# The second bias tile of the attention requested beside the first, and the weight sums of the up pairs built in other halves and one split ahead of their casts

## The chip, the cores and the metric

The kernel runs on one core of one Trainium2 chip. The metric is device time in microseconds (us) of one launch on the slowest core, which here is the only core; several launches are timed and the median is taken. Beside the timed launches one execution is recorded by the hardware profiler, and every duration below that is not a median comes from that execution.

## What is computed

One inference step of a two-layer encoder trunk for 1024 prompt tokens and 32 sample tokens, all in fp32. Layer 0 mixes with an mLSTM, layer 1 with a windowed attention that has a distance bias and one learned sink for each head; after each stands a SwiGLU block, and after each block a layer norm. Cut to what the change touches:

```python
def swiglu(x, w_gu, w_down):
    g, u = jnp.split(x @ w_gu, 2, axis=-1)
    return (jax.nn.silu(g) * u) @ w_down

def sink_attention(q, k, v, sinks, bias):
    s = jnp.einsum('bcqhgd,bckhd->bchgqk', q, k).astype(F32) * (HEAD_DIM ** -0.5) + bias
    sk = sinks.astype(F32).reshape(N_KV_HEADS, GROUP)[:, :, None, None]
    mx = jnp.maximum(jnp.max(s, -1, keepdims=True), sk)
    p = jnp.exp(s - mx)
    p = p / (jnp.sum(p, -1, keepdims=True) + jnp.exp(sk - mx))
    return jnp.einsum('bchgqk,bckhd->bcqhgd', p.astype(v.dtype), v)

def trunk(...):
    ...
        x = layer_norm(DEEPNORM_ALPHA * x + mix, ln_g[layer, 0], ln_b[layer, 0])
        x = layer_norm(DEEPNORM_ALPHA * x + swiglu(x, w_gu[layer], w_down[layer]), ln_g[layer, 1], ln_b[layer, 1])
```

The model width is 1024, the hidden width of SwiGLU 2816 (22 tiles of 128), and there are 16 query heads of 64.

## The kernel before, in words

**Layout and products.** Activations lie transposed: 128 features on the partitions, the 1056 tokens as columns. An fp32 product is made of three TensorE (PE) matmuls: each operand is split into a rounded high part and a low part, and `gemm` (L360) adds high times high (L368), high times low (L369) and low times high (L370) in PSUM.

**Weights.** The class `Weights` (L129) turns weights into such high and low parts. It walks one fixed list of jobs. `load_to` (L156) asks for a raw unit of 128x1024 (tile `wr`, four buffers) by a DMA from SyncE's queue (SP, L162). A job splits one half of a unit: ScalarE (ACT) casts it to the high part (tile `wh`, L208), and GpSimd (POOL), or for some units VectorE (DVE), subtracts to get the low part (tile `wl`, L210). Five pairs of buffers hold the parts. When a product has been issued, `done` (L234) frees its parts and issues the next job, so that four halves stand split or in work ahead of PE.

**The up product.** Of each SwiGLU's 22 hidden tiles, two are done plainly and 20 (`up_tile`, L1342) by a scheme that saves one product in eight: two raw units `a` and `b` (gate and up weights, each with halves 1 and 2) go into seven factors, and each factor is multiplied with an operand of its own (`x11`, `x21`, `t1` to `t4`, `x22`). The factors are a1, a2, b2, s1 = b1 + b2, s2 = s1 - a1, s3 = a1 - b1 and s4 = a2 - s2. Their job order is a1, a2, b2, s2, s1, s3, s4; PE takes them as a1, a2, s2, b2, s1, s3, s4. Four sums of 128x512 on DVE make s1 to s4 in place in the two raw tiles (`_source`, L166): at the job of b2 one (L176), at s2 two (L179 and L180), at s1 one (L182). Each is issued with the job that casts it, and DVE takes its instructions in order. The products go to two PSUM banks A and two B in turn; ACT copies A out (L1362, L1372, L1379, L1390), DVE adds B (L1367, L1375, L1382 to L1384). A product that goes on adding to A waits for the copy before it. The down product's pairs use the same code.

**Staging.** After every second hidden tile a task `stage` (L1278) forms the operands of the down product: DVE sums (L1300, L1301, L1306, L1313), ACT casts (L1288), DVE or POOL subtracts (L1289), SP stores 528 KB to DRAM (L1290, `hs_x` and `hs_t`). There are two buffers for it, so the third cast of a stage waits for the first store.

**Attention.** Eight pairs of heads j visit nine blocks b of 128 tokens. `scores` (L1707) multiplies queries and keys into two PSUM banks `psS` (L1719, L1720), and DVE adds the bias (L1725), whose tile `bt` carries the sink in its last column. ACT takes the exponential (L1737), DVE the reciprocal (L1741), POOL scales (L1743), PE transposes (L1763), ACT and DVE split the result (L1766, L1767), PE multiplies with the values (L1778, L1779). `load_bias` (L1649) asks for the bias of a head pair (two DMAs from SP, L1653 and L1654: 256 KB and a small one) and copies the sinks into it (POOL, L1655 and L1656). The first tile is asked for when the keys begin; each further one when the visit before it begins, with two buffers in turn. The visits are 0, 1, 2, 3 and then 0 to 7.

**Order.** No scheduler reorders anything: each engine runs its instructions in the order in which the code records them, and waits there for what they need. Tasks (`Weave`, L70) are recorded between matmuls by estimated times that stand in the code. SP's queue holds the loads of weights, the stores of the stages, and the copies that spread keys and queries over partitions (L1589 to L1593, L1630, L1631), all in order. Each DMA also waits for the DMA eight before it to land, since eight semaphores are used in turn.

Of the kernel before, what the change touches and what calls it, by code (L numbers as in the profile page):

```python
# [30 lines left out]
FT = D_FF // P  # L31
# [3 lines left out]
FIRST, TAIL = 2, 4  # L35
# [34 lines left out]
class Weave:  # L70


    def __init__(self):
        self.tasks = []
        self.feed = None
# [53 lines left out]
class Weights:  # L129
# [7 lines left out]
    def __init__(self, nc, pool, units, pairs, on_vector):  # L137
        self.nc, self.pool, self.units, self.on_vector = nc, pool, units, on_vector
        self.nload = self.njob = 0
        self.raw, self.parts, self.home, self.live = {}, {}, {}, set()  # L140
        self.jobs, self.last = [], {}
        self.wait, self.ahead, self.pause = 0.0, False, FEED_W
        self.depth = RAW - 1
        self.spare, self.spared = None, set()
        u = 0
        while u < len(units):
            if u in pairs:
                self.jobs += [(u, f) for f in self.FACTORS]
                self.last[u] = self.last[u + 1] = len(self.jobs) - 1
                u += 2  # L150
            else:
                self.jobs += [(u, 0), (u, 1)]
                self.last[u] = len(self.jobs) - 1
                u += 1
# [11 lines left out]
    def _source(self, u, f):  # L166

        n = self.units[u].shape[-1] // 2
        if f in (0, 1):
            return self.raw[u][:, f * n : (f + 1) * n]  # L170
        sub, add = self.nc.vector.tensor_sub, self.nc.vector.tensor_add
        a, b = self.raw[u], self.raw[u + 1]
        a1, a2, b1, b2 = a[:, :n], a[:, n : 2 * n], b[:, :n], b[:, n : 2 * n]
        if f == "b2":

            sub(a1, a1, b1)  # L176
        elif f == "s2":

            add(b1, b1, b2)  # L179
            sub(b2, b2, a1)  # L180
        elif f == "s1":
            sub(a2, a2, b2)  # L182
        return {"a1": a1, "a2": a2, "b2": b2, "s1": b1, "s2": b2, "s3": a1, "s4": a2}[f]

    def _next(self):
        if self.njob == len(self.jobs):
            return False
        key = self.jobs[self.njob]
        u, f = key
        if key not in self.home and len(self.live) == SLOTS and (self.spared or not self.spare):  # L190
            return False
        if key in self.home and any(self.home.get(k) is self.home[key] for k in self.parts):
            return False
        self.load_to(u if f in (0, 1) else u + 1)
        r = self._source(u, f)
        w = r.shape[-1]
        if key in self.home:
            hi, lo = self.home[key]
        else:
            if self.spare and not self.spared:  # L200
                self.spared.add(key)
                at, tag, bufs = self.spare, "x", 1
            else:
                self.live.add(key)
                at, tag, bufs = self.pool, "", SLOTS
            hi = at.tile([P, WD // 2], F32R, name=f"wh{u}_{f}", tag="wh" + tag, bufs=bufs)[:, :w]
            lo = at.tile([P, WD // 2], F32R, name=f"wl{u}_{f}", tag="wl" + tag, bufs=bufs)[:, :w]
        self.nc.scalar.copy(hi, r)  # L208
        eng = self.nc.vector if key in self.on_vector else self.nc.gpsimd
        eng.tensor_sub(lo, r, hi.bitcast(F32))  # L210
        self.parts[key] = (hi, lo)
        self.njob += 1
        if f in (1, "s4"):
            del self.raw[u]
            if f == "s4":
                del self.raw[u + 1]
                u += 1
            self.load_to(u + self.depth)
        return True

    def split_to(self, i):
# [28 lines left out]
def kernel(ctx: ExitStack, tc: tile.TileContext, A, O):  # L250
# [14 lines left out]
    def new(p, tag, shape, dt=F32, bufs=1):  # L265
        uid[0] += 1
        return p.tile(list(shape), dt, name=f"{tag}_{uid[0]}", tag=tag, bufs=bufs)
# [27 lines left out]
    U_UP, U_DN = [], []  # L295
# [25 lines left out]
    on_vector.update((u, f) for u in U_O + U_OUT_A[0] + U_OUT_B[1] for f in range(2))  # L321
    on_vector.update((u, f) for u in U_Q[:1] for f in range(2))
    W = Weights(nc, base, units, pairs, on_vector)
    wv.feed = W.feed


# [52 lines left out]
    def tiles_of(half):  # L379

        hi, lo = half
        return [(hi[:, c : c + P], lo[:, c : c + P]) for c in range(0, hi.shape[-1], P)]

    def wcols(u):
        a, b = W.get(u)
        return tiles_of(a) + tiles_of(b)
# [245 lines left out]
    nc.scalar.preload_act_table_set("natural_log_exp_and_others")  # L632
    W.spare = pa
    eg = ExitStack()
# [943 lines left out]
    def k_part(src, c0, n):  # L1578

        dst = slice(c0, c0 + n)  # L1580
        nc.scalar.copy(KH[0][:, dst], src)
        nc.vector.tensor_sub(KL[0][:, dst], src, KH[0][:, dst].bitcast(F32))
# [63 lines left out]

    B = {}

    def load_bias(j):  # L1649
        at, bufs = (pb2, 1) if j == 5 else (pb, 2)  # L1650
        bt = new(at, "bt", [P, 2, 257], bufs=bufs)
        sb = new(at, "sb", [DEC, 2, 161], bufs=bufs)
        nc.sync.dma_start(bt[:, :, 0:256], A["bias"][:, 2 * j : 2 * j + 2, :])  # L1653
        nc.sync.dma_start(sb[:, :, 0:160], A["bias"][:DEC, 2 * j : 2 * j + 2, 0:160])  # L1654
        nc.gpsimd.tensor_copy(bt[:, :, 256], nsink[:, 2 * j : 2 * j + 2])  # L1655
        nc.gpsimd.tensor_copy(sb[:, :, 160], nsink[:DEC, 2 * j : 2 * j + 2])  # L1656
        B[j] = (bt, sb)

    load_bias(0)
    def keys_values(g):  # L1660
        if g == 2:
            k_part(ck[:], SEQ, P)
        for f, w in ((k_group, U_KV[g > 0][0]), (v_group, U_KV[g > 0][1])):
            f(g)
            if g != 1:
                W.done(w)
# [32 lines left out]
    ast = {"ready": 0, "scored": 0, "placed": 0, "v": 0, "visit": 0}  # L1699
    def attention(gap):  # L1700
        S = {}

        def window(b):

            return (P, 0) if b == 0 else (96, SEQ) if b == 8 else (0, (b - 1) * P)

        def scores(j, b):  # L1707
            _, t0, R, g, off = CH[b]
            if b == 0 or b == 3 and j < 4:
                ast["visit"] += 1  # L1710
                if ast["visit"] < len(visits):
                    load_bias(visits[ast["visit"]])
            s = S[j, b] = {}
            lo, k0 = window(b)
            q, g2, (bt, sb) = Q[j, g], j // 4, B[j]
            tk = slice(off, off + R)
            kc = slice(k0, k0 + 256 - lo)
            for h in range(2):
                nc.tensor.matmul(psS[h][:R, lo:256], q[:, h, tk], KH[g2][:, kc], start=True, stop=False)  # L1719
                nc.tensor.matmul(psS[h][:R, lo:256], q[:, h, tk], KL[g2][:, kc], start=False, stop=True)  # L1720
            p = s["p"] = new(pb2, "s", [P, 2, 257], bufs=4)
            st = s["st"] = new(pb2, "st", [P, 3, 2], bufs=6)
            bias = sb[:, :, :] if b == 8 else bt[:, :, lo:257]
            for h in range(2):
                nc.vector.tensor_tensor_reduce(  # L1725
                    p[:R, h, lo:257], psS[h][:R, lo:257], bias[:R, h], 1.0, 3e38,
                    op0=ALU.add, op1=ALU.min, accum_out=st[:R, 0, h : h + 1],
                )
            ast["scored"] += 1
# [53 lines left out]
        def place(j, b):  # L1783
# [4 lines left out]
            for h in range(2):  # L1788
# [22 lines left out]
    visits = [*range(4), *range(8)]  # L1811
# [6 lines left out]
    for g in range(1, 3):  # L1818
        keys_values(g)
        wv.launch(v_turn(g, 2.5))  # L1820
# [177 lines left out]
```

## Time and profile before

| | us |
|---|---|
| median of three timed launches | 2218.43 (2216.13 to 2218.95) |
| the profiled execution: its own time | 2219.82 |
| the profiled execution: span of its instructions | 2218.0 |
| TensorE busy in the span | 2178.0 |
| VectorE, ScalarE, GpSimd busy | 1468.7, 1002.6, 1020.5 |
| mean granted TensorE clock (1 is full) | 0.997 |
| up products of layer 0 and of layer 1, from and to | 521 to 931, 1554 to 1964 |
| attention, from and to | 1206 to 1427 |

Busy time is the time in which an engine executed an instruction; idle time is put down to what released the instruction that ended it. A row of a timeline gives start, duration, engine, line, operation, and output and inputs by the program's names with buffer numbers left out, then in brackets the engine's idle time before it and its releaser. A `q` behind an engine's name means its queue, where DMAs are issued. Matmuls follow each other in a pipeline, so the start of one to the start of the next counts, not the duration of one.

### The profile page before, as it was taken

Reading aid. Unit: us, or ns where it says so; the run is one execution under the profiler, and the core shown is the slowest. Engines: PE = TensorE matmul, PEld = TensorE weight load, DVE = VectorE, ACT = ScalarE, POOL = GpSimd, SP = SyncE. Lnnn points to the kernel's source line nnn. Section 1 sums busy time; section 2 is a strip of 40 time slices with the busy share of each in tenths; the row PEclk is TensorE's granted clock in tenths of the full one; section 3 lists DMA queues with packets and bytes.
Section 4 is the critical chain, followed back from the end, with each engine's and each line's share of the span. In section 5 each row is a group of like instructions: output and inputs, shape, how many; then the busy total and the mean of one; then the engine's idle time right before and its main releaser. Section 6 shows DMA issues by size and latency. Waiting matters only on the chain.

```text
span 2218.0 us, 44293 instructions
## 1 busy us (share of the span) xinstructions
PE 2178.0 (98%) x17086; PEld 2149.8 (97%) x17086; DVE 1468.7 (66%) x2848; ACT 1002.6 (45%) x2259; POOL 1020.5 (46%) x982
## 2 busy tenths in 40 slices
PE   9999999999999999999998999999999999999997
PEld 9999999999999999999998999899999999999997
DVE  4465677787666665566667678888576666466657
ACT  4443455464344444321245778756444444422125
POOL 2544210004666566544525776600576666554441
PEclk9999999999999999999999999999999999999999
DMA  5221212212443343797515333521244434397712
GB/s 169 78 62 57 57 39 86 89 39 80 153 155 136 137 155 136 248 333 230 175 57 173 108 100 97 155 63 39 103 162 163 135 138 155 129 343 258 243 59 79
DMA packets 174500, 298.10 MB, mean 134 GB/s; under 512 B 18065, under 2 KB 130761, under 8 KB 174289
## 3 DMA queue, kind: packets, MB, share of 16 engines
q1 hardware_dynamic: 169936, 290.94, 39.9%
q10 hardware_dynamic: 4352, 4.33, 0.6%
q8 instruction: 135, 2.21, 0.4%
q14 instruction: 77, 0.62, 0.1%
HBM read 201.80 MB, written 82.94 MB: 128 GB/s over the span
## 4 chain that ended last, share of the span: by engine, by line
PE 61%; DVE 5%; ACT 3%; DMA 2%; issue 2%; POOL 2%; SPq 0%; POOLq 0%; DVEq 0%; ACTq 0%
PE A L368 9%; PE A L370 9%; PE A L369 9%; PE B L368 6%; PE B L369 6%; PE B L370 6%; PE d L368 4%; PE d L370 4%; PE d L369 4%; PE T L1763 1%; POOL s L1743 1%; DMA hs_x<-z 1%; DMA sx<-hs_t 1%; ACT act L471 1%; PE O L1778 1%
## 5 line engine op out<-in xcount | busy, mean ns | idle before, releaser
L210 POOL TENSOR_TENSOR wl_s<-wr,wh_s 128x512 fp32r<-128x512 f32 x224 | 316.6, 1433 | 262.6 <-ACT wh_s L208 187.6
L210 POOL TENSOR_TENSOR wl_a<-wr,wh_a 128x512 fp32r<-128x512 f32 x112 | 168.7, 1513 | 386.7 <-ACT wh_a L208 264.5
L368 PE MATMUL d<-sx,wh 128*128 128x264 f32 (+2 forms) x1068 | 341.3, 320 | 2.1 <-ACT wh L208 1.6
L370 PE MATMUL d<-sx,wl 128*128 128x264 f32 (+2 forms) x1068 | 325.7, 305 | 2.8 <-POOL wl L210 2.8
L369 PE MATMUL d<-sx,wh 128*128 128x264 f32 (+2 forms) x1068 | 324.8, 304 | 0.4 <-DVE sx L399 0.4
L208 ACT CAST wh_s<-wr 128x512 fp32r<-128x512 f32 x224 | 136.0, 619 | 323.4 <-DVE wr L180 295.6
L368 PE MATMUL A<-sx,wh_s 128*128 128x264 f32 x896 | 254.8, 284 | 1.8 <-ACT z L1372 1.8
L369 PE MATMUL A<-sx,wh_s 128*128 128x264 f32 x896 | 254.2, 284 | 0.0
L370 PE MATMUL A<-sx,wl_s 128*128 128x264 f32 x896 | 254.0, 284 | 0.0
L368 PEld LDWEIGHTS d<-sx,wh 128*128 128x128 f32 x1068 | 201.9, 189 | 5.8 <-ACT wh L208 2.3
L370 PEld LDWEIGHTS d<-sx,wl 128*128 128x128 f32 x1068 | 201.3, 189 | 4.2 <-POOL wl L210 3.9
L369 PEld LDWEIGHTS d<-sx,wh 128*128 128x128 f32 x1068 | 202.1, 189 | 1.5 <-DVE sx L399 0.7
L368 PE MATMUL d<-sx,ex 128*128 128x264 f32 x624 | 180.5, 289 | 0.1
L369 PE MATMUL d<-sx,ex 128*128 128x264 f32 x624 | 177.2, 284 | 0.0
L370 PE MATMUL d<-sx,ex 128*128 128x264 f32 x624 | 176.9, 284 | 0.0
L368 PEld LDWEIGHTS A<-sx,wh_s 128*128 128x128 f32 x896 | 168.4, 188 | 2.4 <-ACT z L1372 2.2
L370 PEld LDWEIGHTS A<-sx,wl_s 128*128 128x128 f32 x896 | 168.8, 188 | 0.0
L369 PEld LDWEIGHTS A<-sx,wh_s 128*128 128x128 f32 x896 | 168.4, 188 | 0.0
L1289 POOL TENSOR_TENSOR z<-z 128x528 fp32r<-128x528 f32 x76 | 104.8, 1378 | 113.4 <-ACT z L1288 106.8
L210 POOL TENSOR_TENSOR wl<-wr,wh 128x512 fp32r<-128x512 f32 (+2 forms) x81 | 104.1, 1293 | 93.1 <-ACT wh L208 89.3
L1743 POOL TENSOR_SCALAR s<-s,st 128x256 f32<-128x256 f32 (+1 forms) x144 | 123.1, 867 | 47.9 <-DVE st L1741 32.0
L1288 ACT CAST z<-z 128x528 fp32r<-128x528 f32 x136 | 86.1, 633 | 94.2 <-DVE z L1301 39.1
(348 smaller groups left out, 7307.3 us busy)
## 6 DMA issues: line engine op xcount, KB each, us to landing
wr<-in_gu SPq DMA_DIRECT2D x92, 512.0 KB
hs_x<-z SPq DMA_DIRECT2D x72, 528.0 KB
hs_t<-z SPq DMA_DIRECT2D x64, 528.0 KB
sx<-hs_x SPq DMA_DIRECT2D x112, 264.0 KB
sx<-hs_t SPq DMA_DIRECT2D x64, 264.0 KB
ex<-hs_t SPq DMA_DIRECT2D x64, 264.0 KB
wr<-in_dn SPq DMA_DIRECT2D x32, 512.0 KB
ex<-hs_x SPq DMA_DIRECT2D x32, 264.0 KB
```

The source lines that it names most:

```text
L208: self.nc.scalar.copy(hi, r)
L210: eng.tensor_sub(lo, r, hi.bitcast(F32))
L368: nc.tensor.matmul(out, ah, bh, start=start and k == 0, stop=False, **kw)
L369: nc.tensor.matmul(out, ah, bl, start=False, stop=False, **kw)
L370: nc.tensor.matmul(out, al, bh, start=False, stop=stop and k == last, **kw)
L471: nc.scalar.activation(z, z, AF.Identity, scale=gk, bias=bk)
L1288: nc.scalar.copy(hi.bitcast(F32R), buf(s))
L1289: eng.tensor_sub(lo.bitcast(F32R), buf(s), hi)
L1743: nc.gpsimd.tensor_scalar_mul(p[:R, h, lo:256], p[:R, h, lo:256], st[:R, 2, h : h + 1])
L1763: nc.tensor.transpose(pt[:nk, i, h, :R], p[:R, h, c : c + nk], ident[:R, :R])
L1778: nc.tensor.matmul(po[:, :, :R], v, s["hi"][:nk, i, :, :R], start=(i == 0), stop=False)
```

## The change

The bias tile of visit 1 is asked for right behind that of visit 0, without its sinks; at the beginning of visit 0, where it was asked for before, only the two copies of the sinks are made. Later visits are as before.

For the 20 up pairs of each layer (not for the down pairs) the sums are placed in other halves: s1 = b1 + b2 still in b1, but s2 = s1 - a1 in a1, s3 = b2 - s2 in b2 and s4 = a2 - s2 in a2. Each is issued behind the job before the one that casts it. There are four sums a pair, as before.

```diff
+        if u not in self.early:
+            return self._in_place(u, f, n)
+        self.prepare(u, f)
+        a, b = self.raw[u], self.raw[u + 1]
+        return {
+            "a1": a[:, :n], "a2": a[:, n : 2 * n], "b2": b[:, n : 2 * n],
+            "s1": b[:, :n], "s2": a[:, :n], "s3": b[:, n : 2 * n], "s4": a[:, n : 2 * n],
+        }[f]
+
+    def _in_place(self, u, f, n):
+
         sub, add = self.nc.vector.tensor_sub, self.nc.vector.tensor_add
...
+    def prepare(self, u, f):
+
+        if (u, f) in self.made or f not in ("s2", "s3", "s4"):
+            return
+        self.made.add((u, f))
...
+        if f == "s2":
+            add(b1, b1, b2)
+            sub(a1, b1, a1)
+        elif f == "s3":
+            sub(b2, b2, a1)
+        else:
+            sub(a2, a2, a1)
 
     def _next(self):
...
             self.load_to(u + self.depth)
+        if self.njob < len(self.jobs):
+            u, f = self.jobs[self.njob]
+            if u in self.early and u in self.raw and u + 1 in self.raw:
+                self.prepare(u, f)
         return True
...
     W = Weights(nc, base, units, pairs, on_vector)
+    W.early = {up[i] for up in U_UP for i in range(FIRST, FT)}
...
-    def load_bias(j):
+    def load_bias(j, sinks=True):
+        if j in B:
+            return end_bias(j)
         at, bufs = (pb2, 1) if j == 5 else (pb, 2)
...
+        B[j] = (bt, sb)
+        if sinks:
+            end_bias(j)
+
+    def end_bias(j):
+        bt, sb = B[j]
         nc.gpsimd.tensor_copy(bt[:, :, 256], nsink[:, 2 * j : 2 * j + 2])
         nc.gpsimd.tensor_copy(sb[:, :, 160], nsink[:DEC, 2 * j : 2 * j + 2])
-        B[j] = (bt, sb)
 
     load_bias(0)
+    load_bias(1, False)
...
                 if ast["visit"] < len(visits):
+                    if ast["visit"] > 1:
+                        B.pop(visits[ast["visit"]], None)
                     load_bias(visits[ast["visit"]])
```

The order on PE, ACT and POOL stays as it was, but for the halves that are read. It moves at two places. The first is DVE's queue in the middle of an up product, where the factors of the third pair (raw units `wr42` and `wr43`) are made. Before:

```order
L1313 TENSOR_TENSOR z_627_4631<-z_627_4631 128x528
L176 TENSOR_TENSOR wr42_6618<-wr42_6618,wr43_6620 128x512
L1382 TENSOR_TENSOR z_627_4631<-z_627_4631,B_699_6917 128x528
L1383 TENSOR_TENSOR z_627_4631<-z_627_4631,B_699_6917 128x528
L1384 TENSOR_TENSOR z_627_4631<-z_627_4631 128x528
L179 TENSOR_TENSOR wr43_6620<-wr43_6620 128x512
L180 TENSOR_TENSOR wr43_6620<-wr43_6620,wr42_6618 128x512
L1397 TENSOR_TENSOR z_627_4631<-z_627_4631 128x528
L1289 TENSOR_TENSOR z_627_4631<-z_627_4631 128x528
L182 TENSOR_TENSOR wr42_6618<-wr42_6618,wr43_6620 128x512
```

The same place after the change, where the lines that both kernels have stand 34 further down (L1347 is L1313, L1416 to L1418 are L1382 to L1384, L1431 is L1397, L1323 is L1289, L1334 and L1335 are L1300 and L1301):

```order
L1347 TENSOR_TENSOR z_627_4631<-z_627_4631 128x528
L207 TENSOR_TENSOR wr43_6620<-wr43_6620 128x512
L208 TENSOR_TENSOR wr42_6618<-wr43_6620,wr42_6618 128x512
L1416 TENSOR_TENSOR z_627_4631<-z_627_4631,B_699_6917 128x528
L1417 TENSOR_TENSOR z_627_4631<-z_627_4631,B_699_6917 128x528
L1418 TENSOR_TENSOR z_627_4631<-z_627_4631 128x528
L1431 TENSOR_TENSOR z_627_4631<-z_627_4631 128x528
L1323 TENSOR_TENSOR z_627_4631<-z_627_4631 128x528
L210 TENSOR_TENSOR wr43_6620<-wr43_6620,wr42_6618 128x512
L1334 TENSOR_TENSOR z_627_4631<-z_627_4631 128x528
L1335 TENSOR_TENSOR z_627_4631<-z_627_4631 128x528
L212 TENSOR_TENSOR wr42_6618<-wr42_6618 128x512
```

Both sums that s2 needs (L207 and L208) now stand ahead of the three operations that empty bank B, where only one sum stood; the two that stood behind them are gone, and s3 and s4 (L210, L212) come behind the stage's subtraction.

The second place is SP's queue at the beginning of the keys. Before:

```order
L1639 DMA cv_874_13946<-in_cache_v 128x128
L1653 DMA bt_876_13949<-in_bias 128x2x256
L1654 DMA sb_877_13950<-in_bias 32x2x160
L162 DMA wr108_13997<-in_wkv 128x1024
...
L162 DMA wr113_14305<-in_wqb 128x1024
L1653 DMA bt_906_14350<-in_bias 128x2x256
L1654 DMA sb_907_14351<-in_bias 32x2x160
L1589 DMA KH1_13940<-KH0_13939 64x384
```

After, where L163 is L162, L1689 and L1690 are L1653 and L1654, L1673 is L1639 and L1623 is L1589:

```order
L1673 DMA cv_874_13946<-in_cache_v 128x128
L1689 DMA bt_876_13949<-in_bias 128x2x256
L1690 DMA sb_877_13950<-in_bias 32x2x160
L1689 DMA bt_878_13955<-in_bias 128x2x256
L1690 DMA sb_879_13956<-in_bias 32x2x160
L163 DMA wr108_14001<-in_wkv 128x1024
...
L163 DMA wr113_14309<-in_wqb 128x1024
L1623 DMA KH1_13940<-KH0_13939 64x384
```

The two DMAs of the second bias tile have gone from behind the weight load `wr113` to ahead of the weight load `wr108`, past 28 other DMAs.

More of the change, by code (lines that the diff above doesn't have):

```diff
@@ L143, in __init__ @@
         self.depth = RAW - 1
+        self.made, self.early = set(), set()
         self.spare, self.spared = None, set()
@@ L183, in _source @@
         return {"a1": a1, "a2": a2, "b2": b2, "s1": b1, "s2": b2, "s3": a1, "s4": a2}[f]
+    def prepare(self, u, f):
+        if (u, f) in self.made or f not in ("s2", "s3", "s4"):
+            return
+        self.made.add((u, f))
+        sub, add = self.nc.vector.tensor_sub, self.nc.vector.tensor_add
+        n = self.units[u].shape[-1] // 2
+        a, b = self.raw[u], self.raw[u + 1]
+        a1, a2, b1, b2 = a[:, :n], a[:, n : 2 * n], b[:, :n], b[:, n : 2 * n]
+        if f == "s2":
[5 more added lines that the diff above has]
+            sub(a2, a2, a1)
     def _next(self):
```

## The prediction

> **What bounds the kernel now.** The page comes first, since it says which engine's time is the kernel's time.
>
> ```profile
> PE 2178.0 (98%) x17086; PEld 2149.8 (97%) x17086; DVE 1468.7 (66%) x2848; ACT 1002.6 (45%) x2259; POOL 1020.5 (46%) x982
> ```
>
> PE is busy in 2178.0 of 2218.0 us. PE's own work and its order stay, so only two things can be gained or lost: time in which PE stands still, and time in which its clock is lowered. The waits say who makes PE stand, and whom the two edited engines wait for. Columns: idle us, how often, the longest.
>
> ```profile
> PE psS L1719 <- DVE st L1725: 2.0, 2, 1.8
> PE A L368 <- ACT z L1372: 1.8, 2, 1.3
> ...
> DVE s L1725 <- DMA bt<-in_bias: 3.3, 1, 3.3
> ...
> ACT wh_s L208 <- DVE wr L180: 295.6, 54, 7.5
> ```
>
> The first row and the third belong together: once, DVE waited 3.3 us for a bias tile, and PE 1.8 us for DVE. The second and the fourth belong together too: ACT's casts wait for DVE's second sum of s2 (L180), and PE waits for ACT's copies of bank A, which stand behind those casts. These are the two places of the change; the timeline shows each.
>
> **First part: the bias tile.** Start, duration, engine, and in brackets the idle time before:
>
> ```profile
> 1169.85 0.47 SPq L1654 DMA_DIRECT2D sb<-in_bias  x1
> 1175.80 0.34 SPq L162 DMA_DIRECT2D wr<-in_wkv  x1
> ...
> 1209.38 1.38 SPq L1653 DMA_DIRECT2D bt<-in_bias  x1
> ...
> 1211.33 0.17 DVE L1741 RECIPROCAL st<-st 128x2 f32<-128x2 f32 x1 [0.57 <-ACT s L1737]
> 1214.83 0.29 DVE L1725 CUSTOM_DVE_ANT_0 s<-psS,bt 128x129 f32<-128x129 f32 x1 [3.34 <-DMA bt<-in_bias]
> ...
> 1213.03 0.34 PE L370 MATMUL d<-sx,wl 128*128 128x384 f32 x1
> 1215.19 0.39 PE L1719 MATMUL psS<-KH,Q 128*128 128x256 f32 x1 [1.82 <-DVE st L1725]
> ...
> 1216.40 1.05 PE L1763 MATMUL T<-ident,s 128*128 128x128 f32 x4
> ...
> 1209.65 3.76 POOL L1743 TENSOR_SCALAR s<-s,st 128x256 f32<-128x256 f32 x4
> ```
>
> The tile of visit 1 was asked for at 1209.38, behind the query copies, and DVE used it at 1214.83. DVE had been free since 1211.50, and PE ran out of work at 1213.03 + 0.34 = 1213.37. In the changed kernel the tile is asked for right after 1169.85, 39.5 us sooner. SP issued nothing from 1170.32 to 1175.80, so the two new issues (at most 1.38 + 0.47 us by the old place's rows; 0.47 is what the same small issue took here) fit into that gap and delay none of the weight loads behind them; should they have to wait for an older DMA to land, 5.5 us are there before `wr` at 1175.80, which is what queues behind them. At the old place the copies of keys behind them start some 2 us sooner. The two bias additions then run at about 1211.5 and end by 1211.5 + 2 x 0.29 = 1212.1, which is 1.3 us before PE needs the bank. **Term 1: 1.82 us.**
>
> The clock is the second loss there. Columns: stretch, its length, busy us (count) of PE, weight loads, DVE, ACT, POOL, then the granted clock, DMA share, GB/s.
>
> ```profile
> 1211.40:1215.20 3.80, 1.86 (x13) 1.52 (x12) 0.46 (x4) 0.62 (x2) 2.15 (x5) 1.00 0.79 239
> 1215.20:1219.60 4.40, 4.40 (x22) 4.30 (x23) 3.56 (x14) 3.25 (x12) 1.18 (x2) 0.61 0.40 115
> 1226.40:1229.80 3.40, 1.67 (x13) 1.24 (x11) 1.83 (x9) 3.33 (x12) 2.44 (x3) 1.00 0.23 14
> 1229.80:1233.20 3.40, 3.40 (x15) 3.38 (x16) 1.87 (x9) 1.44 (x6) 3.08 (x3) 0.50 0.66 228
> ```
>
> Twice, PE was busy in about half of a stretch (1.86 of 3.80, 1.67 of 3.40), and the stretch behind it had a low clock (0.61, 0.50). In the first pair the emptiness is this stall. Without it PE would be busy there nearly throughout, so I expect no lowering. PE was busy in all 4.40 us, so the cost was (1 - 0.61) x 4.40 = **term 2: 1.72 us**. The second pair has another cause and stays. Bounds: 0 (the clock falls anyway) to 1.72.
>
> The Trainium skill, page "TensorE: Matmul & The Clock Gate", Part 1, section "What you observe", puts the fall to half clock after at least one idle window of some 3.4 us. The trace differs: here 1.82 us of idling was followed by it. By the page's rule this stall would not be the cause, term 2 would be 0, and the time would be that of rival B.
>
> **Second part: the sums of the up pairs.** Each of seven factors takes PE 24 matmuls. An undisturbed one, by PE's starts, takes 571.43 - 568.52 = 2.91 us.
>
> ```profile
> 527.10 0.39 PE L368 MATMUL A<-ex,wh_s 128*128 128x264 f32 x1
> ...
> 530.62 0.28 PE L368 MATMUL B<-ex,wh_b 128*128 128x264 f32 x1
> ...
> 568.52 0.28 PE L368 MATMUL A<-ex,wh_s 128*128 128x264 f32 x1
> ...
> 571.43 0.28 PE L368 MATMUL B<-ex,wh_b 128*128 128x264 f32 x1
> ...
> 575.84 0.39 PE L368 MATMUL A<-sx,wh_s 128*128 128x264 f32 x1 [1.34 <-ACT z L1372]
> ...
> 1556.59 0.29 PE L368 MATMUL B<-sx,wh_a 128*128 128x264 f32 x1
> ...
> 1559.91 0.39 PE L368 MATMUL A<-ex,wh_s 128*128 128x264 f32 x1 [0.24 <-ACT z L1362]
> ...
> 1563.44 0.28 PE L368 MATMUL B<-ex,wh_b 128*128 128x264 f32 x1
> ...
> 1604.28 0.28 PE L368 MATMUL B<-ex,wh_b 128*128 128x264 f32 x1
> ...
> 1607.78 0.39 PE L368 MATMUL A<-sx,wh_s 128*128 128x264 f32 x1 [0.43 <-ACT z L1372]
> ```
>
> Five factors of both layers took longer: 3.52, 4.41, 3.32, 3.53 and 3.50 us, which is 0.61 + 1.50 + 0.41 + 0.62 + 0.59 = 3.73 us more than 2.91 each. The brackets name 2.01 of it; the rest hides in the modelled ends of pipelined matmuls, so I take the starts. How the largest came about:
>
> ```profile
> 561.34 0.68 DVE L176 TENSOR_TENSOR wr<-wr,wr 128x512 f32<-128x512 f32 x1
> ...
> 562.55 0.69 DVE L1383 TENSOR_TENSOR z<-z,B 128x528 f32<-128x528 f32 x1
> ...
> 564.58 0.69 DVE L180 TENSOR_TENSOR wr<-wr,wr 128x512 f32<-128x512 f32 x1
> 566.52 1.40 DVE L1397 TENSOR_TENSOR z<-z 128x528 f32<-128x528 f32 x1 [1.25 <-ACT z L1390]
> ...
> 562.57 0.28 PE L370 MATMUL A<-sx,wl_s 128*128 128x264 f32 x1
> ...
> 565.36 0.62 ACT L208 CAST wh_s<-wr 128x512 fp32r<-128x512 f32 x1 [6.64 <-DVE wr L180]
> 565.88 0.60 ACT L1390 ACTIVATE z<-A 128x528 f32<-128x528 f32 x1
> ...
> 574.14 0.63 ACT L1288 CAST z<-z 128x528 fp32r<-128x528 f32 x1 [0.76 <-DMA hs_t<-z]
> ...
> 575.20 0.59 ACT L1372 COPY z<-A 128x528 f32<-128x528 f32 x1
> ...
> 569.66 4.40 SPq L1290 DMA_DIRECT2D hs_t<-z  x2
> ```
>
> ACT's cast of s2 (565.36) waited for L180. L1390, which DVE's L1397 needs, waited behind that cast. DVE was late with the operand that SP stored at 569.66, the stage's third cast (574.14) waited for that store, and the copy that PE needed (575.20) stood behind it. In the changed kernel both sums stand where L176 stood: 561.34 + 2 x 0.69 = 562.7 instead of 564.58 + 0.69 = 565.27. So the cast can start 2.5 us sooner, and the chain needs only 1.50. L1390 also needs the last matmul of s4, which began at 562.57, so it can follow the cast at about 563.3 instead of 565.88. The other four stalls are of the same kind and smaller. **Term 3: 3.73 us**, bounds 0 and 3.73.
>
> What is added: nothing, four sums a pair as before. What is late next: the three operations that empty bank B (L1382 to L1384) come one sum later, 0.7 us, and the next product into that bank starts only at 571.43. The sums s3 and s4 now go in places where nothing waits for them within a factor.
>
> **Sum.** 1.82 + 1.72 + 3.73 = 7.27 us. The profiled execution took 2219.82; it would take 2212.55. It stands 1.39 above the median of the three runs, so the median by the sum is 2211.16. I forecast **2211.8**, between the two, since three runs spread over 2.8 us.
>
> **The rivals.**
>
> *B: the clock falls anyway* (term 2 is not gained, 2211.8 + 1.7 = 2213.5). For it: the second pair of windows fell after only 1.73 us of emptiness in small pieces, so other small gaps may be enough. Against it: over the whole span the mean clock is 0.997, so it does not fall often, and both times the emptiness was nearly half of the stretch.
>
> *C: another wait takes the bias's place* (terms 1 and 2 lost, 2215.3). Candidates are POOL's scaling, which ended at 1213.41, or ACT's exponentials. Against it: with PE 1.82 us sooner, its transposes would come at 1216.40 - 1.82 = 1214.58, and POOL is done 1.2 us ahead of that.
>
> *D: ACT stays held* (term 3 lost, 2215.5). For it: the cast at 574.14 waits for a landing that takes 4.40 us, and if another link than DVE sets the store's time, the stall stays. Against it: all links ahead of the store shift, as worked out.
>
> *E: neither part acts*: the median of before, 2218.4.
>
> *F: slower, by DVE.* Two sums ahead of the evictions instead of one, and sums that meet POOL's work are not always short:
>
> ```profile
> L182 DVE TENSOR_TENSOR wr<-wr,wr 128x512 f32<-128x512 f32 x56 | 83.9, 1499 | 0.1
> ...
> L180 DVE TENSOR_TENSOR wr<-wr,wr 128x512 f32<-128x512 f32 x56 | 38.8, 693 | 6.2 <-DVE wr L179 0.5
> ```
>
> The same sum takes 0.69 us at L180 and 1.50 at L182, where POOL splits beside it. If both new sums take 1.50, bank B is emptied 2 x 1.50 - 0.68 = 2.3 us later; it decides from where DVE is more than 8 us behind (from 562.55 + 0.69 = 563.24, when L1383 had read bank B out, to 571.43). Should DVE be so late that each of 40 tiles loses 0.3 us, that is 12 us, and the time 2218.4 + 12 - 3.5 (terms 1 and 2 stay) = 2226.9. Against it: DVE still idled 1.25 us ahead of 566.52, and over the span it is busy for 66%.
>
> The Trainium skill, page "SBUF — State Buffer", section "Who interferes with whom", speaks for F: a DVE operation with two SBUF inputs and a GpSimd operation that reads SBUF lock each other out. The rows agree in kind (1.50 against 0.69 us); by the rule the sums at the new places may wait for whole POOL splits, which stays under the 8 us.
>
> **How the numbers follow.** All three terms: 0.54 (2211.8). B 0.11 (2213.5), C 0.10 (2215.3), D 0.10 (2215.5), E 0.05 (2218.4), F 0.10 (2226.9). A difference of 0.2%, 4.4 us, is about what a measurement of this kernel can tell from no change; the border of faster is 2214.0. Faster: the forecast and B, 0.65. Same: C, D and E, 0.25. Slower: F, 0.10. The range runs from 2209.0 (the sum, and 2 us of scatter as in the runs of before) to 2216.0, which holds B, C and D; E and F stay out, 0.15.
>
> **What would show it.** Right: in the profile after, DVE's row "waits for bt" and PE's 1.8 us behind it are gone, and the clock at about 1215 to 1219 is 1.00; ACT's wait for DVE's sum of s2 falls well below 295.6; all up factors take 2.91 us. Wrong: a new row of PE waiting for DVE on bank B with dozens of occurrences (F), a POOL or ACT row at about 1214 (C), a cast that still waits for `hs_t` with PE behind it (D), a clock below 1 with no stall ahead of it (B).

## The result, and the profile after

| | before | after |
|---|---|---|
| median, us | 2218.41 (2216.13 to 2220.19, 8 runs) | 2212.19 (2209.96 to 2213.98, 8 runs) |
| ratio | | 0.9972, 95% interval 0.9963 to 0.9981 |
| the profiled execution: time; span | 2219.82; 2218.0 | 2213.98; 2212.2 |

The kernel is 0.28% faster, 6.2 us, and the interval does not reach 1, which would be no change. The profiled execution of after happens to be the longest of its eight.

The waits of PE and ACT in the changed kernel (waiting line, what it waited for, us in total, times, longest):

```profile
PE O L1736 <- DVE VR L1679: 3.3, 2, 2.8
...
PE psS L1763 <- DVE st L1769: 0.2, 1, 0.2
...
ACT wh_s L237 <- DVE wr L192: 102.7, 14, 7.5
...
ACT wh_s L237 <- DVE wr L208: 24.1, 8, 4.1
```

The wait of PE for the scores' bank has shrunk from 2.0 to 0.2 us. ACT waited 295.6 us for L180 before, of which 102.7 us (L192) remain in the down pairs, which are unchanged, and 24.1 us for the new sum L208. PE no longer waits for ACT in the up products at all. The first row, a wait for the parts of the values (`VR`) ahead of the attention, is new in its size; it is taken up with after_again below.

The bias place in the timeline:

```profile
1167.51 0.43 SPq L1689 DMA_DIRECT2D bt<-in_bias  x1
1167.98 0.47 SPq L1690 DMA_DIRECT2D sb<-in_bias  x1
1172.93 0.34 SPq L163 DMA_DIRECT2D wr<-in_wkv  x1
...
1212.12 0.17 DVE L1785 RECIPROCAL st<-st 128x2 f32<-128x2 f32 x1 [0.57 <-ACT s L1781]
1212.24 0.29 DVE L1769 CUSTOM_DVE_ANT_0 s<-psS,bt 128x129 f32<-128x129 f32 x1
...
1213.84 0.34 PE L404 MATMUL d<-sx,wl 128*128 128x384 f32 x1
1214.01 0.28 PE L1763 MATMUL psS<-KH,Q 128*128 128x256 f32 x1
```

Both new DMAs (1167.51 and 1167.98) lie in the gap of SP, the bias addition follows the reciprocal at once, and PE goes from its last product straight to the scores.

The same place of the up product that the prediction followed, about 1.5 us earlier in the span (559.88 for 561.34):

```profile
559.88 0.68 DVE L207 TENSOR_TENSOR wr<-wr 128x512 f32<-128x512 f32 x1
560.59 0.69 DVE L208 TENSOR_TENSOR wr<-wr,wr 128x512 f32<-128x512 f32 x1
...
562.43 1.53 DVE L1418 TENSOR_TENSOR z<-z 128x528 f32<-128x528 f32 x1
563.88 1.79 DVE L1431 TENSOR_TENSOR z<-z 128x528 f32<-128x528 f32 x1
...
561.39 0.62 ACT L237 CAST wh_s<-wr 128x512 fp32r<-128x512 f32 x1 [4.13 <-DVE wr L208]
561.92 0.60 ACT L1424 ACTIVATE z<-A 128x528 f32<-128x528 f32 x1
...
564.35 0.60 ACT L1396 COPY z<-A 128x528 f32<-128x528 f32 x1 [0.79 <-PE A L404]
...
571.10 0.59 ACT L1406 COPY z<-A 128x528 f32<-128x528 f32 x1
...
566.32 4.40 SPq L1324 DMA_DIRECT2D hs_t<-z  x2
...
569.98 0.28 PE L402 MATMUL B<-ex,wh_b 128*128 128x264 f32 x1
...
572.88 0.28 PE L402 MATMUL A<-sx,wh_s 128*128 128x264 f32 x1
```

The cast of s2 starts 0.8 us after L208 has started, the copy L1424 right after it, the store goes out at 566.32 instead of 569.66 (3.3 us sooner, of which 1.5 are the earlier span), and the factor that took 4.41 us takes 572.88 - 569.98 = 2.90.

PE's matmuls come in the same order in all these kernels, so the start of one and the same matmul can be subtracted between two profiles. This gives where the time went, stage by stage (us against the first profile of before; the places are its times; negative is a gain; the last three columns are the second profiles of after and before and a kernel of the experiments):

| stage | after | after, 2nd | before, 2nd | old_halves |
|---|---|---|---|---|
| start to 521 | -0.80 | -0.33 | -0.24 | -0.49 |
| up products of layer 0, 521 to 931 | -2.24 | -2.24 | +0.16 | -2.23 |
| 931 to 1185 | +0.19 | +0.18 | -0.01 | +0.02 |
| first keys and queries, 1185 to 1204.9 | +3.67 | +1.68 | +1.23 | +1.02 |
| to the scores behind the bias, 1215.2 | -2.00 | -2.01 | -0.65 | -1.99 |
| to 1233.6 | -3.24 | -3.24 | -3.13 | -3.24 |
| rest of the attention and after it, to 1554 | +0.62 | -0.01 | +1.76 | +0.23 |
| up products of layer 1, 1554 to 1964 | -1.69 | -1.69 | -0.01 | -1.69 |
| to 2207 | -0.34 | -0.50 | -0.44 | -0.63 |

Against the first profile of before the up products gain 2.24 + 1.69 = 3.93 us in every profile with the new order. Among the profiles with the old order they vary by 0.8 us: before_again takes 0.16 us more there, bias_only 0.62 less. The stages of 1185 to 1233.6 hold the bias and also large shifts that the kernel before shows between two of its own executions (+1.23, -0.65, -3.13).

In part these shifts are stretches at half clock. The windows view of four places (length, busy us and count of PE, PEld, DVE, ACT, POOL, then clock, DMA share, GB/s); first profile of before:

```profile
1212.73:1216.15 3.42, 1.60 (x11) 1.28 (x11) 1.18 (x6) 0.96 (x5) 0.93 (x3) 1.00 0.86 259
1216.15:1219.56 3.41, 3.41 (x17) 3.31 (x16) 2.71 (x11) 2.29 (x8) 1.18 (x2) 0.50 0.31 79
```

Second profile of before, at the same stall and ahead of it:

```profile
1197.76:1201.17 3.41, 1.66 (x9) 1.29 (x10) 3.41 (x5) 2.85 (x6) 2.37 (x2) 1.00 1.05 291
1201.17:1204.58 3.41, 2.85 (x11) 2.34 (x10) 2.37 (x7) 2.69 (x9) 2.90 (x4) 0.50 0.56 130
...
1211.41:1214.82 3.41, 2.97 (x18) 2.35 (x17) 0.59 (x2) 1.57 (x5) 3.26 (x6) 1.00 0.81 243
1214.82:1218.24 3.42, 2.56 (x20) 2.53 (x21) 2.65 (x13) 2.03 (x8) 1.19 (x2) 1.00 0.70 186
1218.24:1221.65 3.41, 3.41 (x31) 3.41 (x29) 2.96 (x12) 2.73 (x11) 1.82 (x2) 1.00 0.03 9
```

After:

```profile
1198.89:1202.31 3.42, 0.62 (x4) 0.30 (x2) 1.60 (x7) 2.07 (x6) 3.12 (x3) 1.00 0.89 260
1202.31:1205.72 3.41, 3.41 (x11) 3.41 (x12) 0.43 (x2) 0.78 (x2) 3.34 (x5) 0.50 1.01 269
```

In the second profile of before the bias stall is there, but its rest is divided between two windows, PE is busy for 2.97 and 2.56 us of them, and no half clock follows. The half clock came 15 us earlier (1201.17 for 1216.15), ahead of the attention. After has one there too, behind its wait of 2.8 us, and one at 1417: two stretches, as many as in the first profile of before.

### The profile page after: what moved, and what is told of

Its sections match the earlier page's. It is cut to its first block, busy times and chain, and to the rows that moved or that the text cites. A ratio compares the mean times of both kernels' runs of the same rounds, so it can differ in the third digit from the quotient of the medians.

```text
span 2212.2 us, 44257 instructions
## 1 busy us (share of the span) xinstructions
PE 2175.5 (98%) x17086; PEld 2149.4 (97%) x17086; DVE 1455.2 (66%) x2848; ACT 1007.9 (46%) x2259; POOL 989.8 (45%) x982
## 4 chain that ended last, share of the span: by engine, by line
PE 85%; DVE 6%; DMA 3%; ACT 3%; issue 1%; POOL 1%; SPq 0%; ACTq 0%; POOLq 0%; DVEq 0%
PE d L402 10%; PE d L404 10%; PE d L403 10%; PE A L402 9%; PE A L404 9%; PE A L403 9%; PE B L402 7%; PE B L403 7%; PE B L404 7%; DMA sx<-hs_t 1%; PE T L1807 1%; ACT act L505 1%; DMA hs_x<-z 1%; POOL s L1787 1%; PE T L955 1%
## 5 line engine op out<-in xcount | busy, mean ns | idle before, releaser
L239 POOL TENSOR_TENSOR wl_s<-wr,wh_s 128x512 fp32r<-128x512 f32 x224 | 304.1, 1367 | 237.4 <-ACT wh_s L237 168.9
L239 POOL TENSOR_TENSOR wl_a<-wr,wh_a 128x512 fp32r<-128x512 f32 x112 | 153.5, 1373 | 409.4 <-ACT wh_a L237 288.2
L237 ACT CAST wh_s<-wr 128x512 fp32r<-128x512 f32 x224 | 135.7, 618 | 192.6 <-DVE wr L192 102.7
L1323 POOL TENSOR_TENSOR z<-z 128x528 fp32r<-128x528 f32 x76 | 103.2, 1357 | 126.8 <-ACT z L1322 113.3
L402 PE MATMUL A<-ex,wh_s 128*128 128x264 f32 x448 | 127.5, 285 | 0.0
```

The costliest lines, as they stand in the source:

```text
L402: nc.tensor.matmul(out, ah, bh, start=start and k == 0, stop=False, **kw)
L1323: eng.tensor_sub(lo.bitcast(F32R), buf(s), hi)
```

## The experiments

Twelve kernels ran, each in comparison with the kernel before on the same chip. Ratios are against it.

| kernel | median, us | ratio, 95% interval |
|---|---|---|
| after_again | 2212.16 | 0.9978 (0.9969 to 0.9987) |
| bias_only | 2215.29 | 0.9990 (0.9981 to 0.9999) |
| sums_only | 2213.39 | 0.9980 (0.9971 to 0.9989) |
| before_again (one run) | 2218.58 | |
| not_ahead | 2220.46 | 1.0014 (1.0005 to 1.0023) |
| old_halves | 2212.34 | 0.9976 (0.9966 to 0.9986) |
| extra4 | 2221.28 | 1.0013 (1.0004 to 1.0022) |
| fill | 2212.42 | 0.9976 (0.9967 to 0.9985) |
| lead_s2 | 2217.66 | 0.9995 (0.9986 to 1.0004) |
| lead_s34 | 2214.55 | 0.9980 (0.9972 to 0.9989) |
| extra2 | 2214.22 | 0.9981 (0.9973 to 0.9990) |
| fill2 | 2215.69 | 0.9989 (0.9980 to 0.9998) |

The runs of before beside them had medians of 2217.8, 2217.87 and 2218.19 us.

**Both kernels again (after_again, before_again).** No edit.

> The changed kernel once more, for a second profile. In its first profile the up products gained 2.24 + 1.69 us, the bias stall's 1.9 us were gone, and two stretches of 3.41 us at half clock stood at about 1202 and 1417 us of the span instead of 1216 and 1230. Theory H (a half-clock stretch is caused by the emptiness of PE just ahead of it and lands where the phase of a running window of 3.41 us lets it): up products and the bias place are as in the first profile, the number of half-clock stretches is anything from 0 to 4 and at least one of them stands elsewhere; the time lies within 2 us of 2212.2. Rival P (the stretches belong to places of the program): they stand at the same matmuls as in the first profile of the changed kernel.

> The kernel before once more, for a second profile. Theory H: the five long up factors and the wait for bt come again within 0.1 us each, but the half-clock stretches need not stand at 1216 and 1230 us; waits in the query product (1190 to 1204 us, 4.3 us in the first profile) differ by a us or two from one execution to the next. Rival P: half-clock stretches at the same matmuls, the query product's waits the same.

Measured: the up products and the bias place repeat within 0.2 us (0.13 for the largest factor, more than the 0.1 that was expected), but for the bias stall of before, which is 1.18 us instead of 1.82. The half-clock stretches moved: 1216 and 1230 in the first profile of before, 1201 and 1420 to 1426 in the second; 1202 and 1417 in the first of after, 1196 to 1203 in the second. What follows: rival P falls as it was worded, since the stretches do not stand at the same matmuls in each execution. They do not fall just anywhere either. In the 14 profiles there are 28, 13 of them between 1195 and 1208 us (in all but the first profile of before), 1 at 1216, 7 between 1225 and 1233, 7 between 1416 and 1426; which of these a given execution has is what changes. The wait of 2.8 us in the first profile of after is in none of the other 13 profiles, where it is 0.6 us or less. ACT, which casts the values, waited there for a DMA of the queries for 0.70 us ahead of that cast; why that was so, and what made up the rest, stays open.

**One part alone (bias_only, sums_only).**

```diff
-    W.early = {up[i] for up in U_UP for i in range(FIRST, FT)}
+    W.early = set()
```

```diff
-    load_bias(1, False)
+    pass
```

> The changed kernel with the up sums as before; only the bias tile of visit 1 is asked for early. Terms 1 and 2 of the prediction: 2218.4 - 3.5 = 2214.9. If term 2 is given back by half-clock stretches elsewhere: 2218.4 - 1.8 = 2216.6. If another wait takes the bias's place: 2218.4. In the profile: no wait of DVE for bt, PE's psS wait under 0.3 us, the five long up factors of before unchanged (3.7 us in all).

> The changed kernel with the bias tile of visit 1 asked for where it was before; only the up sums are changed. Term 3 of the prediction: 2218.4 - 3.7 = 2214.7, all up factors at 2.91 us. If the gain in layer 0 is lost again because the query product waits for its weights whatever PE does before it (in the first profile of the changed kernel 2.8 us were waited there): about 2218.4 - 1.7 = 2216.7. DVE waits for bt as before, over 3 us.

Measured: bias_only gains 2.5 us (2217.8 - 2215.29), sums_only 4.4, together 6.9 against 5.6 for both in the same comparison; each median is uncertain by about 2 us. With 2217.8 as the time of before, bias_only was expected at 2214.3 if the half clock is gained and at 2216.0 if not; 2215.29 lies between, so the medians do not decide that. Its long factors of the up products add up to 3.3 us, where 3.7 were expected. In bias_only PE starts the scores 2.00 us sooner by the stages, as in after. In sums_only DVE waits for `bt` for 2.5 us, not over 3, the bias stall is 0.92 us, and no half clock follows it. The up products gain 3.93 us in sums_only, and its median, 2213.39, is below the 2214.7 that was expected and well below the 2216.7 of the rival, so the gain of layer 0 is not lost behind it.

**The place of the sums and their halves (not_ahead, old_halves, lead_s2, lead_s34).** In not_ahead the call in `_next` is left out; in lead_s2 and lead_s34 it is made for some sums only:

```diff
-                self.prepare(u, f)
+                pass
```

```diff
-            if u in self.early and u in self.raw and u + 1 in self.raw:
+            if f == "s2" and u in self.early and u in self.raw and u + 1 in self.raw:
```

(`f != "s2"` in lead_s34.) In old_halves the up pairs use `_in_place` as before, and its sums of s2 are issued behind the job of b2:

```diff
-        if u not in self.early:
+        if u not in self.early or True:
...
-        elif f == "s2":
+        elif f == "s2" and (u, f) not in self.made:
+            self.made.add((u, f))
...
-                self.prepare(u, f)
+                if f == "s2":
+                    self._source(u, f)
```

> The changed kernel, with each sum issued with the job that casts it again, but in the other halves. DVE then empties bank B first and makes both sums of s2 behind it, so these come one sum (0.65 us) sooner than in the kernel before and 2 us later than in the changed one. Theory O (what counts is that ACT's cast of s2 no longer holds up the copy behind it, so the place of the sums): the largest long factor shrinks from 4.41 to about 3.8 us, the up products keep some 2 of the 3.9 us that the change gained, the time is about 2214.2. Rival X (the other halves do it, by sparing waits on POOL's splits): all factors at 2.91 us, 2212.2.

> The changed kernel with the sums of the up pairs in the halves of the kernel before, but the two sums of s2 issued behind the job of b2, ahead of the emptying of bank B. Three sums then stand there instead of two, the last of them waiting for POOL's split of b2, which had ended 0.5 us before that place in the kernel before. Theory O: s2 is ready 0.7 us later than in the changed kernel and 1.8 us sooner than before; all factors at 2.91 us or the largest at most 0.3 us over; 2212.2 to 2212.7. Rival X (the halves are needed, since the wait for POOL's split holds DVE): the up gain is lost, 2215 to 2216 or more.

> The changed kernel, in which only the two sums of s2 are issued ahead; s3 and s4 come with the jobs that cast them, in the other halves. Theory O (any sum for which ACT's cast has to wait holds up the copy of bank A behind it): the long factors at the beginning of each up product (0.84 and 0.49 us in the run without any lead) are gone, the 14 of 0.35 to 0.81 us behind s4's cast stay; the up products lose about 3.7 + 3.7 us against the changed kernel, 2219 to 2220. Rival (only the sums of s2 matter): 2212.2.

> The changed kernel, in which the sums of s3 and s4 are issued ahead and those of s2 with the job that casts it. Theory O: only the long factors at the beginning of each up product are left (0.84 + 0.49 us in the run without any lead), 2213 to 2214. Rival (only the sums of s2 matter): the gain of the up products is lost, 2216 or more.

Measured, by the stages of the up products (both layers together, against after): not_ahead loses 8.7 us, lead_s2 6.3, lead_s34 2.5, old_halves 0.0; the medians say 8.3, 5.5, 2.4 and 0.2. Lead_s2's loss and lead_s34's add up to that of not_ahead. Lead_s2 came out below the 2219 to 2220 that were expected and lead_s34 above the 2213 to 2214, each nearer to that than to its rival. Not_ahead came out by neither expectation: both had the other halves harmless by themselves. The timeline of not_ahead, in the next tile:

```profile
592.51 0.71 DVE L1347 TENSOR_TENSOR z<-z 128x528 f32<-128x528 f32 x1 [2.73 <-POOL z L1323]
593.13 0.68 DVE L212 TENSOR_TENSOR wr<-wr 128x512 f32<-128x512 f32 x1
...
593.90 0.62 ACT L237 CAST wh_s<-wr 128x512 fp32r<-128x512 f32 x1 [2.92 <-DVE wr L212]
594.43 0.59 ACT L1406 COPY z<-A 128x528 f32<-128x528 f32 x1
...
595.08 0.39 PE L402 MATMUL A<-sx,wh_s 128*128 128x264 f32 x1 [0.65 <-ACT z L1406]
```

Here it is the sum of s4 (L212). It stands behind a stage sum that waits for POOL, ACT's cast waits for it for 2.92 us, and the copy of bank A comes late. In the waits of not_ahead PE stands for that copy 14 times:

```profile
PE A L402 <- ACT z L1406: 3.6, 14, 0.6
```

It is the mechanism of the prediction with another sum in it. With s2 alone made ahead the same wait is there, as often:

```profile
PE A L402 <- ACT z L1406: 2.6, 14, 0.2
```

In the kernel before, s3 was made at b2 and s4 at s1, so neither came late; with the other halves each needs its lead.

In old_halves, DVE's sum waits for POOL's split of b2, which the other halves avoid:

```profile
L192 DVE TENSOR_TENSOR wr<-wr,wr 128x512 f32<-128x512 f32 x56 | 53.9, 963 | 79.6 <-POOL wl_b L239 76.9
```

These 76.9 us of waiting reach nothing that PE waits for: the up products are as long as in after, to 0.01 us. So the lead of the sums of s2 makes the gain; the halves need not change for it.

**More work ahead of the evictions (extra4, extra2).** Shown for extra4; extra2 has `range(1)`:

```diff
             add(b1, b1, b2)
             sub(a1, b1, a1)
+            for _ in range(2):
+                add(b1, b1, b2)
+                sub(b1, b1, b2)
```

> The changed kernel, in which behind the sums of s2 of each up pair b2 is added to s1 and taken off again twice: four more sums of 128x512 ahead of the emptying of bank B, 2.8 us by the undisturbed duration and up to 6 beside POOL. It is case F of the prediction made on purpose. By the margin of 8.2 us: bank B costs nothing; the stage's store comes 2.5 us later or more, and since ACT's copy had some 1.2 us to spare in the changed kernel, the long factors of the kernel before come back; 2213 to 2217. If DVE's place ahead of the evictions is sharper than that: each of 40 pairs loses some 0.5 us or more, 2232 or more.

> The changed kernel with two more sums of 128x512 in each up pair ahead of the emptying of bank B (b2 added to s1 and taken off again). In the run with four, ACT's copy of bank A waited until DVE had emptied B and PE stood 1.3 us behind it at 571 us; by its times and those of the changed kernel there are about 4.9 us between the end of the emptying in the changed kernel and the point from which PE waits. Two sums are 1.4 us, up to 3 beside POOL, so: no long factor, 2212 to 2213. Rival (each added sum ahead of the emptying costs, so half of what four cost): 2216 to 2217.

Measured: four sums cost 9.1 us, two 2.0. Both are between the expectations. The up products of extra4 lose 8.7 us, all in three pairs of each layer and not in all 40: the first loses 2.0 to 2.1 us, the third 1.7 and the fourth 0.6, with single factors of up to 4.5 us. The timeline of the third pair:

```profile
563.84 0.69 DVE L210 TENSOR_TENSOR wr<-wr 128x512 f32<-128x512 f32 x1
...
565.29 1.67 DVE L210 TENSOR_TENSOR wr<-wr 128x512 f32<-128x512 f32 x1
...
568.84 1.50 DVE L1421 TENSOR_TENSOR z<-z 128x528 f32<-128x528 f32 x1
...
570.42 0.60 ACT L1399 COPY z<-A 128x528 f32<-128x528 f32 x1 [2.02 <-DVE z L1421]
...
571.07 0.39 PE L405 MATMUL A<-ex,wh_s 128*128 128x264 f32 x1 [1.32 <-ACT z L1399]
```

ACT's next copy (L1399, that is L1396 of after) writes into `z`, which the last eviction (L1421) still reads. So in this pair DVE's lateness reaches PE through ACT and bank A, long before bank B is written again. In the first pair of each layer it does reach PE through bank B. There the added sums stand ahead of DVE's reading of the bank that the plain tile before used and that B takes over:

```profile
PE B L405 <- DVE z L1371: 2.2, 2, 1.2
```

For the third pair the margin can be worked out. In after, L1418 ends at 563.96; the product that this copy delays starts at 569.98 - 2.91 = 567.07, and the copy must start 0.65 us ahead of it: the margin is some 2.4 us. The 4.9 us of the expectation of extra2 compared times of two kernels that stand 2.5 us apart there. In extra2 that place holds, but the first pair of each layer is 0.7 and 0.5 us longer, since the added sums write s1 once more:

```profile
ACT wh_s L240 <- DVE wr L211: 1.8, 2, 1.0
```

ACT's cast of s1 waits for them twice, and that is a cost of the experiment, not of the change.

**The clock (fill, fill2).** Matmuls whose result is overwritten, ahead of the product that waits for its weights:

```diff
         ps = psdense(g)
+        for _ in range(8 if u == U_KV[1][0] and g == 1 else 0):
+            nc.tensor.matmul(ps, sxh[0][g][:, :P], sxh[0][g][:], start=True, stop=True)
         gemm(ps, wcols(u), xcols(g))
```

Fill2 has 12 of them, and in `gemm`, ahead of the first low part, 6 more into bank `psS`:

```diff
+            while k == 0 and filler:
+                for _ in range(6):
+                    nc.tensor.matmul(filler[0], sxh[0][0][:, :P], sxh[0][0][:, :256], start=True, stop=True)
+                filler.pop()
```

> The changed kernel with 8 matmuls of 128x384 more (1.4 us), whose result is overwritten, ahead of the first product of the second group of keys, where PE waited 2.33 us for its weights in four of six profiles. Theory H, sharpened by the six profiles (on a fixed grid of 3.41 us, the stretch behind one in which PE was busy for less than half runs at half clock): the stretch with that wait rises from 0.18 to 0.49 busy to over 0.6, no half-clock stretch stands between 1190 and 1206 us, and the time falls by 0.5 to 2 us against the changed kernel, to 2210.2 to 2211.7. Rival P (the clock falls at this place of the program whatever PE does): half clock between 1195 and 1203 us as before, and 2212.2.

> The changed kernel with 12 overwritten matmuls of 128x384 (2.1 us) ahead of the first product of the second group of keys and 6 of 128x256 (0.7 us) ahead of its first low part. In the run with 8, two rests of 0.9 us still fell into one stretch of the 3.41 us grid (busy 0.45), and the next ran at half clock. Theory H: all stretches between 1190 and 1203 us are over 0.55 busy, none runs at half clock, and the time falls by 0.8 to 1.7 us to 2210.5 to 2211.4. Rival P (the place): half clock between 1195 and 1203 us again, 2212.2.

Measured: neither did what it was meant to, and both missed the times that theory H gave (2212.42 and 2215.69). In fill, two rests of 0.91 and 0.97 us fell into one window, in which PE was busy for 1.52 us:

```profile
1194.50:1197.90 3.40, 1.52 (x8) 0.89 (x6) 2.78 (x6) 3.40 (x8) 1.65 (x2) 1.00 1.02 307
1197.90:1201.30 3.40, 3.40 (x12) 3.23 (x13) 1.98 (x7) 2.52 (x7) 3.40 (x3) 0.50 0.57 185
```

In fill2 the added matmuls themselves had to wait, for DVE to clear a column of that bank, and the stretch at half clock came behind this wait, at 1201.7:

```profile
1200.46 0.98 PE L407 MATMUL psS<-sx 128*128 128x256 f32 x6 [2.96 <-DVE psS L1734]
```

So the cause was not shown by taking a stretch away, and fill came out at the time and with the half clock that rival P gave. What the 14 profiles show together: all half-clock stretches start on a grid of 3.413 us, to 0.001 us within a profile. Take PE's busy share of each window of that grid from its instructions, and leave out the end of the launch from 2195 us on. Of the windows at full clock, 20 were busy for a share of 0.50 or less, and the window behind each ran at half clock; of 19 between 0.52 and 0.61, 8 were followed by one; none of those busy for 0.61 or more was. At the end of the launch there is an exception: in lead_s2 a window busy for 0.46 (from 2204.88) was followed by one at full clock. Five of the 28 stretches also last for a second window, though PE was busy for 0.71 to 0.96 of the first; the share does not say why. This is an agreement over profiles, not an experiment on the cause.

## Why the prediction was right, and where it was not

**Term 1, the bias stall, 1.82 us: right.** PE starts the scores 2.00 us sooner against the first profile of before. The size is that of one profile, though. The stall itself varies: 1.82, 1.18 and 0.92 us in the three profiles that have it, as the tile lands. The issues at the new place cost nothing, as worked out.

**Term 2, the half clock, 1.72 us: wrong.** The step that failed is "Without it PE would be busy there nearly throughout, so I expect no lowering", put into the sum as a gain. The lowering did go from that place, but the place was chance: it depends on how the grid of windows cuts the rests of PE, and this differs from one execution to the next. Before_again and sums_only have the stall and no half clock behind it; after has two stretches elsewhere. Counted in windows of 3.41 us, the eleven profiles with the bias early have one to three at half clock, the two of before have two and three, sums_only has four. The timed runs agree: their mean granted clock is 0.9966 over 26 runs of before, 0.9970 over the 8 of after and 0.9965 over the 10 of after_again, and one window at half clock is worth 3.41 x 0.5 / 2218 = 0.0008. So at most a part of the term was gained on average. The mechanism of rival B held, that the clock falls anyway, and its time was 2213.5. The size of the term was right for a window that does fall there: the two of before between 1215.2 and 1233.6 make 3.24 us.

**Term 3, the up products, 3.73 us: right.** They gained 2.24 + 1.69 = 3.93 us against the first profile of before, 4.1 and 3.3 against the two others with the old order (before_again and bias_only). All long factors are gone, and the chain from L208 over the cast, the copy and the store is the one that was followed. Its condition, that ACT's cast does not wait long, is what lead_s2 and lead_s34 test: where one of the sums comes late, the loss is back. What the prediction did not see is how this depends on s3 and s4. It said that nothing waits for them within a factor; that holds with the lead, and without it they cost 6.3 us.

**The sum.** Without term 2 it is 1.82 + 3.73 = 5.55 us, and the median 2218.43 - 5.55 = 2212.9. The forecast of 2211.8 lay between the sum taken from the profiled execution and from the median; measured were 2212.19 and 2212.16. The two right terms, as measured against the first profile of before, are 2.0 + 3.9 = 5.9 us, and the medians differ by 6.2 and 5.6. That the forecast came within 0.4 us is in part luck: a term of 1.72 us was gained in part at most, but 0.64 of the 7.27 had been taken off for the scatter of the runs, 0.4 came from the two other terms being larger than forecast, and the rest is within what medians and profiles of one kernel differ by.

**Rivals C, D and E** fell: no wait took the bias's place (psS 0.2 us), the cast behind the store no longer holds PE, and both parts act alone. **Rival F** did not occur, but its point was mis-sized. It gave DVE 8.2 us, until bank B is written again; extra4 shows some 2.4 us in the third pair, through ACT's copy, which waits for the last eviction, and in the first pair a bank B that PE does wait for. One pair pays up to 2.1 us there, but only three pairs of a layer pay.

The Trainium skill, page "TensorE: Matmul & The Clock Gate", Part 1, section "What's actually happening", has a free-running window of 3413 ns, so that where the change of clock falls depends on the phase. The grid of 3.413 us measured here agrees. The table of the two states, which stands in the same section and not in "What you observe", asks for an idle window ahead of half clock; here windows with PE busy for 0.18 to 0.50 were still followed by it, and up to 0.61 sometimes.

## What to carry to other kernels

Where an engine in order both prepares operands and empties results, a late operand delays the results queued behind it: give the sum its lead, and check every other sum that the new layout moves. A buffer's margin is the shortest way back to the bound engine, through any engine that shares a tile with the late one, not only the next write of the same buffer. A lowered clock behind one stall of a single profile is not a gain to count: take a second profile of the same kernel first.

## What the runs showed of the hardware

In the 14 profiles the lowering of the clock comes in whole windows of 3.413 us on a grid that runs on through the launch. All 20 windows ahead of the end of the launch in which PE was busy for half or less were followed by one at half clock; they all start between 1192 and 1226 us, and at the end of the launch there is one exception (lead_s2). One window at half clock cost 0.8 to 1.2 us in the stage of the first keys and queries, where PE also waits for weights (the +1.23 and +1.02 of the table are two of six such profiles), and some 1.6 us where PE is the bound (most of the -3.24 between 1215.2 and 1233.6 are the two of before). Between 1416 and 1426 it hardly shows: the stage of 1233.6 to 1554 is 0.09 to 0.62 us longer than in the first profile of before in the profiles with one such window there, and -0.19 to +0.32 in those without.

A DVE sum of 128x512 lasts 0.69 us, or up to about a microsecond more where POOL works beside it: in the timeline of extra4 above, one instruction of the added loop (L210) took 0.69 us in the first turn and 1.67 in the second, at 565.29, while a split ran on POOL from 564.62 for 1.80 us.
